# Splitting 784 token columns as 512 + 272 instead of 384 + 400 in the input projection of a hybrid encoder

## The chip, the cores and the metric

The kernel runs on one core of a Trainium2 chip. The metric is the device time of one execution in microseconds (us); the value for the kernel before is the median of three runs.

## The reference

One encoder layer is applied to two groups of tokens, a prompt of 1024 tokens and a sample of 256 tokens; each is preceded by the same 16 learned meta tokens. The model width is 2048, a head has 128 channels. All arrays are float32.

```python
u = rms_norm(h, norm_w) @ w_in                      # (tokens, 2048) x (2048, 6656)
qa, ka, va, za, qb, kb, vb, zb = jnp.split(u, split_points(), axis=-1)
qa = apply_axial_rope(rms_norm(qa, q_norm_a), rope_tabs)   # 8 heads
ka = apply_axial_rope(rms_norm(ka, k_norm_a), rope_tabs)   # 2 key/value heads
ya = global_gqa(qa, ka, va) * jax.nn.silu(za)
qb, kb = rms_norm(qb, q_norm_b), rms_norm(kb, k_norm_b)    # 8 heads
yb = neighbourhood_attention(qb, kb, vb, rpb) * jax.nn.silu(zb)
return h + jnp.concatenate([ya, yb], axis=-1) @ w_out      # (tokens, 2048) x (2048, 2048)
```

`global_gqa` is full softmax attention of one group over itself. `neighbourhood_attention` lets each token of a 64-column grid see a window of 8 rows by 16 columns with a learned bias, and the meta tokens.

## The kernel before, in words

**Number format.** Each float32 operand of a large product is split into two parts, a rounded high part and the rest, both of type float32r. A product is the sum of three matmuls: high times high, high times low, low times high. In the projection these are lines 199, 200 and 201 of `strips`, which take `wh` and `xh`, `wh` and `xl`, `wl` and `xh`. A weight tile of 128 x 128 is the stationary operand, a block of token columns of x the moving one, and the result goes to a PSUM tile (`pp`) with the 128 output channels on the partitions and the tokens along the row.

**Two chunks of tokens.** The 16 meta tokens, the 1024 prompt tokens and the 256 sample tokens are projected as two chunks. Chunk 1 holds 512 columns (256 of the sample, the first 240 of the prompt, 16 meta), chunk 2 the other T2 = 784 prompt tokens. Channels lie on the partitions, so an x tile is 128 channels by the chunk's tokens, and 16 such tiles (KT) make the 2048 channels.

**Strips.** The 6656 output channels are 52 strips of 128. `strips` projects one strip (or two together): for each of the 16 x tiles, for each block of token columns, three matmuls. In chunk 1 a strip has one block of 512 columns (keys, values) or of 496 (queries, gates, without the meta tokens). In chunk 2 a strip has two blocks, from the list `BL` in `chunk2`, and so two PSUM tiles of up to 512 columns:

```python
BL = [(0, NB), (NB, T2 - NB)]       # line 664; NB = 384: columns 0..384 and 384..784
```

When the strip is done, an evacuation reads both PSUM tiles, block after block: `qk_evac` (norm over the channels by an all-reduce on GpSimd, optional rope, split), `v_rows` and `rows_out` (128-column transposes on TensorE, copies, stores) or `z_evac` (silu). Intermediate tiles come from the pool `ev`, which has 8 buffers in chunk 2.

**x in chunk 2.** While chunk 1 is projected, the raw x of chunk 2 is copied to a DRAM buffer `x2d` and its squares are summed. `load_all_x` then opens chunk 2: for each of the 16 tiles one DMA on SP's queue (line 147) brings 784 columns into the place of the low part, ScalarE writes the high part (line 149), VectorE overwrites the place with the low part (line 150). The order of the tiles' places (3, 4, 0, 1, 2, 5, ...) follows the memory of chunk 1, which they take over. A tile is `[128, 2, 800]` with its start at a multiple of 128 bytes: the high part at column 0, the low part at column 800, and a block is the slice `xh[:, o:o + n]` or `xl[:, o:o + n]` of these.

**Order of the work.** Chunk 1 interleaves its strips with the attention of the sample. Chunk 2 runs the global heads first (for each head a gate strip, a query strip, four attention blocks of 256 queries, and one strip of the local heads as filling), then the other local strips between the blocks of the neighbourhood attention. The last four blocks run beside the beginning of the output projection, which works on two halves of 640 tokens as blocks of 320 columns (lines 915 to 917), and whose order is held as written. Elsewhere a planner with a timeline of estimated costs sets the order of the instructions on each engine, with a raised priority for the weight loads (`woff`); the DMAs of x in chunk 2 are held back behind the weight loads of the 48th strip (`early`).

Of the kernel before, what the change touches and what calls it, by code (L numbers as in the profile page):

```python
# [12 lines left out]
F32 = mybir.dt.float32  # L13
F32R = mybir.dt.float32r
AF = mybir.ActivationFunctionType
ALU = mybir.AluOpType
# [4 lines left out]
P = 128  # L21
DM = 2048
KT = 16
# [4 lines left out]
C1P = 240  # L28
T1 = NMETA + NS + C1P
T2 = NP - C1P  # L30
TX = 800
NB = 384
ALIGN = 128
NH = 8
EPS = 1e-6
# [13 lines left out]
class Kern:  # L49
# [39 lines left out]
    def get_x(self, kt):  # L89

        nc = self.nc
        if kt not in self.xs:
            for i in range(kt, kt + 3):
                self.load_x(i)
            r = self.xraw[kt]
            t = self.x.tile([P, 2, T1], F32R, tag="x", name="x", align_bytes=ALIGN)
            h, l = t[:, 0, :], t[:, 1, :]
            w = self.nw[:, kt:kt + 1]
            nc.scalar.activation(h, r, AF.Copy, scale=w)
            nc.vector.scalar_tensor_tensor(out=l, in0=r, scalar=w, in1=h.bitcast(F32), op0=ALU.mult, op1=ALU.subtract)  # L100
            if kt >= LAG:
                self.square(kt - LAG)
            self.xs[kt] = (h, l)
            if kt == KT - 1:
                for d, c in self.consts:
                    nc.sync.dma_start(d, c)
                nc.scalar.mul(self.nqkw[:], self.qkw[:], -1.0)
                for i in range(KT - LAG, KT):
                    self.square(i)
                self.token_scale(*self.scale, T1)  # L110
        return self.xs[kt]
# [26 lines left out]
    def load_all_x(self):  # L138


        nc = self.nc
        t = [self.x.tile([P, 2, TX], F32R, tag="x", name="x", align_bytes=ALIGN) for _ in range(KT)]
        for kt, i in enumerate((3, 4, 0, 1, 2, *range(5, KT))):
            h, l = t[i][:, 0, :T2], t[i][:, 1, :T2]
            r = l.bitcast(F32)
            with self.tc.issue_after(self.early):
                nc.sync.dma_start(r, self.x2d[kt][:])
            w = self.nw[:, kt:kt + 1]
            nc.scalar.activation(h, r, AF.Copy, scale=w)
            nc.vector.scalar_tensor_tensor(out=l, in0=r, scalar=w, in1=h.bitcast(F32), op0=ALU.mult, op1=ALU.subtract)  # L150
            self.xs[kt] = (h, l)
        for d, c in self.consts:
            nc.sync.dma_start(d, c)

# [11 lines left out]
    def strips(self, jobs, getx):  # L166


        nc, tc = self.nc, self.tc
        out = [[pool.tile([P, 512], F32, tag=tag, name="pp") for pool, tag in pools] for _, _, pools in jobs]  # L170
        for c in range(KT // WCH):
            ws = []
            for s, _, _ in jobs:
                with tc.high_priority(offset=self.woff):
                    w = self.raw.tile([P, WCH, P], F32, tag="raw", name="wr")
                    single = self.projected == 2 and c == 0 and not self.second
                    for i in range(0, WCH, 1 if single else WCH):
                        e = i + (1 if single else WCH)
                        self.lastw = nc.sync.dma_start(w[:, i:e], self.io["w_in"][s][:, c * WCH + i:c * WCH + e, :]).ins
                    wh = self.w.tile([P, WCH, P], F32R, tag="wh", name="wh")  # L180
                    wl = self.w.tile([P, WCH, P], F32R, tag="wl", name="wl")
                    if self.second and s not in AGAIN:
                        nc.sync.dma_start(wl[:].bitcast(F32), self.wld[s][:, c * WCH:(c + 1) * WCH, :])
                        nc.scalar.copy(wh[:], w[:])  # L184
                    else:
                        for i in range(0, WCH, 1 if single else WCH):
                            e = i + (1 if single else WCH)
                            self.lastsplit = self.split(wh[:, i:e], wl[:, i:e], w[:, i:e])
                            self.lasthi = self.hi
                ws.append((wh, wl))  # L190
                if not self.second and s not in AGAIN:
                    nc.sync.dma_start(self.wld[s][:, c * WCH:(c + 1) * WCH, :], wl[:].bitcast(F32))
            for k in range(WCH):
                kt = c * WCH + k
                xh, xl = getx(kt)
                for (wh, wl), ps, (_, blocks, _) in zip(ws, out, jobs):
                    for p, (o, n) in zip(ps, blocks):
                        first, last = kt == 0, kt == KT - 1
                        nc.tensor.matmul(p[:, :n], wh[:, k, :], xh[:, o:o + n], start=first, stop=False)  # L199
                        nc.tensor.matmul(p[:, :n], wh[:, k, :], xl[:, o:o + n], start=False, stop=False)  # L200
                        nc.tensor.matmul(p[:, :n], wl[:, k, :], xh[:, o:o + n], start=False, stop=last)  # L201
        return out

    def qk_evac(self, ps, o, n, wc, rope, segs):
# [266 lines left out]
    def rows_out(self, vt, n, dst, o):  # L471

        nc = self.nc
        for a in range(0, n, 4 * P):
            offs = range(a, min(n, a + 4 * P), P)
            full = [x for x in offs if x + P <= n]
            t = self.ev.tile([P, 3, P], F32, tag="ev", name="vl")
            tp = self.tp.tile([P, 4, P], F32, tag="tp", name="tp")
            for i, x in enumerate(offs):
                m = min(P, n - x)  # L480
                nc.tensor.transpose(tp[:m, i, :], vt[:, x:x + m], self.ident[:])
            f = len(full)
            nc.scalar.copy(t[:, :f, :], tp[:, :f, :])
            nc.sync.dma_start(dst[o + a:o + a + P * f].rearrange("(t p) d -> p t d", p=P), t[:, :f, :])
            if f < len(offs):
                m = n - offs[f]
                t = self.ev.tile([m, P], F32, tag="ev", name="vl")
                nc.scalar.copy(t[:], tp[:m, f, :])
                nc.sync.dma_start(dst[o + n - m:o + n], t[:])
# [165 lines left out]
    def chunk2(self):  # L655
# [7 lines left out]
        self.load_all_x()  # L663
        BL = [(0, NB), (NB, T2 - NB)]

# [491 lines left out]
```

## Time and profile before

| | |
|---|---|
| time, median of 3 runs | 2230.27 us (2229.54 to 2231.46) |
| profiled execution | 2232.76 us, of which its span is 2231.0 us |
| TensorE matmul busy | 2207.4 us, 99%, 13064 instructions |
| weight loads busy (beside the matmuls) | 2101.0 us, 94% |
| VectorE (DVE) busy | 1644.2 us, 74% |
| ScalarE (ACT) busy | 1127.5 us, 51% |
| GpSimd (POOL) busy | 531.2 us, 24% |
| DMA | 391.21 MB, mean 175 GB/s |
| granted TensorE clock, mean | 0.996 |

Busy time is the union of an engine's instructions as the profiler has them. Matmuls overlap: each is recorded from its start to the end of its last write, so a mean duration of 344 ns doesn't say that the next one starts 344 ns later. How fast TensorE goes is read from the start times in the timeline. In a group's row, "x832" is the number of instructions, the number after the bar is busy time in us and then the mean duration in ns, and after the second bar stand the idle time of the engine before them and what ended it. The span begins with chunk 1 (to about 625 us); chunk 2 lasts to about 1810 us, and the output projection ends the kernel.

### The profile page before, as it was taken

The numbers are of one execution on the slowest core, as the hardware profiler recorded it, in microseconds if no ns is written. First come the engines' busy times: TensorE is split into PE (matmuls) and PEld (weight loads), VectorE is DVE, ScalarE is ACT, GpSimd is POOL, SyncE is SP. The second block draws the span as 40 slices with busy tenths as digits, with TensorE's granted clock in tenths as the row PEclk, the third lists the DMA queues.
The fourth block names the chain that finished last, engine by engine and source line by source line (L and its number), as shares of the span: only waits on it lengthen the run. The fifth ranks groups of instructions, "written<-read, shape, count | busy, mean of one in ns | idle before, by whom it ended". The sixth has DMA issues, their size and how long they took to land.

```text
span 2231.0 us, 36738 instructions
## 1 busy us (share of the span) xinstructions
PE 2207.4 (99%) x13064; PEld 2101.0 (94%) x13064; DVE 1644.2 (74%) x2895; ACT 1127.5 (51%) x2288; POOL 531.2 (24%) x249
## 2 busy tenths in 40 slices
PE   8999999999999999999999999999999999999999
PEld 6888788888899999999999999999999999999999
DVE  7687876788855998994898998567668766536743
ACT  6555454455554676764676665444434454232220
POOL 1232421122211332331232233322422322000000
PEclk9999999999999999999999999999999999999999
DMA  8767899998464333334333336544343464745663
GB/s 287 222 192 223 272 310 312 323 299 297 143 219 144 101 104 114 95 118 140 101 106 114 105 110 206 158 139 143 117 132 109 136 221 140 230 148 161 201 211 111
DMA packets 267480, 391.21 MB, mean 175 GB/s; under 512 B 46720, under 2 KB 126496, under 8 KB 267296
## 3 DMA queue, kind: packets, MB, share of 16 engines
q1 hardware_dynamic: 267296, 388.86, 54.1%
q8 instruction: 102, 1.67, 0.3%
q14 instruction: 82, 0.67, 0.1%
HBM read 286.19 MB, written 102.42 MB: 174 GB/s over the span
## 4 chain that ended last, share of the span: by engine, by line
PE 89%; DVE 4%; DMA 3%; issue 1%; ACT 1%; SPq 1%; POOL 0%; DVEq 0%; ACTq 0%; POOLq 0%
PE pp L199 19%; PE pp L200 19%; PE pp L201 19%; PE pq L916 6%; PE pq L917 6%; PE pq L915 6%; PE po L460 2%; PE sp L321 1%; PE sp L322 1%; PE sp L323 1%; PE po L363 1%; PE po L361 1%; PE po L362 1%; DVE wl L56 1%; PE sp L428 1%
## 5 line engine op out<-in xcount | busy, mean ns | idle before, releaser
L199 PE MATMUL pp<-x,wh 128*128 128x384 f32 (+2 forms) x2496 | 896.3, 360 | 7.0 <-ACT wh L55 7.0
L200 PE MATMUL pp<-x,wh 128*128 128x384 f32 (+2 forms) x2496 | 893.7, 358 | 0.0
L201 PE MATMUL pp<-x,wl 128*128 128x384 f32 (+2 forms) x2496 | 889.3, 356 | 0.2 <-DVE wl L56 0.2
L199 PEld LDWEIGHTS pp<-x,wh 128*128 128x128 f32 x2496 | 469.6, 188 | 38.1 <-ACT wh L55 8.4
L201 PEld LDWEIGHTS pp<-x,wl 128*128 128x128 f32 x2496 | 470.2, 188 | 30.1 <-DVE wl L56 1.0
L200 PEld LDWEIGHTS pp<-x,wh 128*128 128x128 f32 x2496 | 470.1, 188 | 30.1 <-DVE x L150 0.5
L56 DVE TENSOR_TENSOR wl<-wr,wh 128x512 fp32r<-128x512 f32 (+1 forms) x402 | 288.6, 730 | 130.3 <-ACT wh L55 108.8
L55 ACT CAST wh<-wr 128x512 fp32r<-128x512 f32 (+1 forms) x402 | 239.7, 610 | 227.1 <-PE pp L200 164.8
L209 POOL PARTITION_ALL_REDUCE m<-ms x78 | 224.3, 2875 | 410.8 <-ACT ms L207 356.2
L290 POOL PARTITION_ALL_REDUCE tot<-a x80 | 186.7, 2334 | 469.7 <-DVE a L288 453.3
L916 PE MATMUL pq<-ym,wh 128*128 128x320 f32 x896 | 278.6, 311 | 2.0 <-DVE ym L56 1.9
L915 PE MATMUL pq<-ym,wh 128*128 128x320 f32 x896 | 278.8, 311 | 1.3 <-ACT ym L55 0.9
L917 PE MATMUL pq<-ym,wl 128*128 128x320 f32 x896 | 278.1, 310 | 0.0
L273 POOL PARTITION_ALL_REDUCE ma<-m x80 | 111.1, 1388 | 421.7 <-DVE m L271 419.1
L916 PEld LDWEIGHTS pq<-ym,wh 128*128 128x128 f32 x896 | 169.8, 189 | 2.8 <-DVE ym L56 2.8
L915 PEld LDWEIGHTS pq<-ym,wh 128*128 128x128 f32 x896 | 169.7, 190 | 2.2 <-ACT ym L55 1.5
L917 PEld LDWEIGHTS pq<-ym,wl 128*128 128x128 f32 x896 | 169.7, 189 | 0.3 <-DVE wl L56 0.3
L341 DVE TENSOR_TENSOR S<-S,ma 128x512 f32<-128x512 f32 x136 | 104.0, 820 | 8.1 <-POOL ma L273 7.7
L56 DVE TENSOR_TENSOR pl<-S,ph 128x512 fp32r<-128x512 f32 x136 | 100.1, 748 | 10.4 <-ACT ph L55 10.0
L325 ACT COPY S<-sp 128x512 f32<-128x512 f32 x136 | 78.1, 580 | 55.4 <-PE sp L323 42.5
L184 ACT CAST wh<-wr 128x512 fp32r<-128x512 f32 x132 | 81.3, 616 | 45.1 <-PE pp L200 43.4
L342 ACT ACTIVATE S<-S 128x512 f32<-128x512 f32 x136 | 83.6, 629 | 36.3 <-DVE S L341 36.2
(207 smaller groups left out, 3306.6 us busy)
## 6 DMA issues: line engine op xcount, KB each, us to landing
wr<-in_w_in SPq DMA_DIRECT2D x414, 256.0 KB, 3.7
wld<-wl SPq DMA_DIRECT2D x132, 256.0 KB, 4.5
wl<-wld SPq DMA_DIRECT2D x132, 256.0 KB, 3.2
wq<-in_w_out SPq DMA_DIRECT2D x64, 256.0 KB, 5.6
td<-wq SPq DMA_DIRECT2D x64, 256.0 KB, 4.3
wr<-td SPq DMA_DIRECT2D x64, 256.0 KB, 3.3
yr<-yd SPq DMA_DIRECT2D x48, 320.0 KB, 3.9
wr<-in_w_out SPq DMA_DIRECT2D x48, 256.0 KB, 4.1
```

What stands on the lines that cost most here:

```text
L55: self.hi = nc.scalar.copy(hi, full).ins
L56: return nc.vector.tensor_tensor(out=lo, in0=full, in1=hi.bitcast(F32), op=ALU.subtract).ins
L199: nc.tensor.matmul(p[:, :n], wh[:, k, :], xh[:, o:o + n], start=first, stop=False)
L200: nc.tensor.matmul(p[:, :n], wh[:, k, :], xl[:, o:o + n], start=False, stop=False)
L201: nc.tensor.matmul(p[:, :n], wl[:, k, :], xh[:, o:o + n], start=False, stop=last)
L209: nc.gpsimd.partition_all_reduce(m2[:], ms[:], P, RED.add)
L273: nc.gpsimd.partition_all_reduce(ma[:], m1[:], P, RED.max)
L290: nc.gpsimd.partition_all_reduce(tot[:], a1[:], P, RED.add)
L341: nc.vector.tensor_tensor(out=s, in0=s, in1=mb, op=ALU.subtract)
L915: nc.tensor.matmul(ps[:, b, :B], wh, yh[:, o], start=k == 0, stop=False)
L916: nc.tensor.matmul(ps[:, b, :B], wh, yl[:, o], start=False, stop=False)
L917: nc.tensor.matmul(ps[:, b, :B], wl, yh[:, o], start=False, stop=k == 7)
```

## The change

The two blocks of a strip in chunk 2 become 512 and 272 columns. A tile of x in chunk 2 is laid out by block: the high part of the first block at column 0, its low part at 512, the high part of the second at 1024, its low part at 1312; the row has 1584 columns instead of 1600. `load_all_x` makes each tile in two pieces, one per block, each with its own DMA, its own ScalarE copy and its own VectorE subtraction. `strips` takes a list of (high, low) pairs, one per block, instead of slicing by the offset. The tile into which `rows_out` copies its transposes holds four columns of 128 instead of three. The widest tile of the `ev` pool in chunk 2 goes from 400 columns to 512.

```diff
-TX = 800
-NB = 384
+NB = 512
+XLAY = ((0, 512, 512), (1024, 1312, 272))
+TX = 1584
...
-            self.xs[kt] = (h, l)
+            self.xs[kt] = [(h, l)]
...
-        t = [self.x.tile([P, 2, TX], F32R, tag="x", name="x", align_bytes=ALIGN) for _ in range(KT)]
+        t = [self.x.tile([P, TX], F32R, tag="x", name="x", align_bytes=ALIGN) for _ in range(KT)]
         for kt, i in enumerate((3, 4, 0, 1, 2, *range(5, KT))):
-            h, l = t[i][:, 0, :T2], t[i][:, 1, :T2]
-            r = l.bitcast(F32)
-            with self.tc.issue_after(self.early):
-                nc.sync.dma_start(r, self.x2d[kt][:])
             w = self.nw[:, kt:kt + 1]
-            nc.scalar.activation(h, r, AF.Copy, scale=w)
-            nc.vector.scalar_tensor_tensor(out=l, in0=r, scalar=w, in1=h.bitcast(F32), op0=ALU.mult, op1=ALU.subtract)
-            self.xs[kt] = (h, l)
+            self.xs[kt] = []
+            o = 0
+            for a, b, n in XLAY:
+                h, l = t[i][:, a:a + n], t[i][:, b:b + n]
+                r = l.bitcast(F32)
+                with self.tc.issue_after(self.early):
+                    nc.sync.dma_start(r, self.x2d[kt][:, o:o + n])
+                nc.scalar.activation(h, r, AF.Copy, scale=w)
+                nc.vector.scalar_tensor_tensor(out=l, in0=r, scalar=w, in1=h.bitcast(F32), op0=ALU.mult, op1=ALU.subtract)
+                self.xs[kt].append((h, l))
+                o += n
...
-                xh, xl = getx(kt)
+                x = getx(kt)
                 for (wh, wl), ps, (_, blocks, _) in zip(ws, out, jobs):
-                    for p, (o, n) in zip(ps, blocks):
+                    for p, (_, n), (xh, xl) in zip(ps, blocks, x):
                         first, last = kt == 0, kt == KT - 1
-                        nc.tensor.matmul(p[:, :n], wh[:, k, :], xh[:, o:o + n], start=first, stop=False)
-                        nc.tensor.matmul(p[:, :n], wh[:, k, :], xl[:, o:o + n], start=False, stop=False)
-                        nc.tensor.matmul(p[:, :n], wl[:, k, :], xh[:, o:o + n], start=False, stop=last)
+                        nc.tensor.matmul(p[:, :n], wh[:, k, :], xh[:, :n], start=first, stop=False)
+                        nc.tensor.matmul(p[:, :n], wh[:, k, :], xl[:, :n], start=False, stop=False)
+                        nc.tensor.matmul(p[:, :n], wl[:, k, :], xh[:, :n], start=False, stop=last)
...
-            t = self.ev.tile([P, 3, P], F32, tag="ev", name="vl")
+            t = self.ev.tile([P, 4, P], F32, tag="ev", name="vl")
```

## The prediction

> **What bounds the kernel now.** I read the page first: engine totals, the chain that ended last, and the costliest group.
>
> ```profile
> span 2231.0 us, 36738 instructions
> PE 2207.4 (99%) x13064; PEld 2101.0 (94%) x13064; DVE 1644.2 (74%) x2895; ACT 1127.5 (51%) x2288; POOL 531.2 (24%) x249
> ...
> PE 89%; DVE 4%; DMA 3%; issue 1%; ACT 1%; SPq 1%; POOL 0%; DVEq 0%; ACTq 0%; POOLq 0%
> ...
> L199 PE MATMUL pp<-x,wh 128*128 128x384 f32 (+2 forms) x2496 | 896.3, 360 | 7.0 <-ACT wh L55 7.0
> ```
>
> The tensor engine is named busy for 99% of the span and carries 89% of the last chain. "Busy" alone doesn't prove that it streams, since matmul ends are modelled. So I took the busy time of each engine by stage, and then the waits of PE inside the stretch where only the second chunk is projected and attended (650 to 1805 us).
>
> ```profile
> 620.00:650.00 30.00, 28.52 (x160) 27.28 (x158) 24.82 (x40) 21.93 (x36) 3.67 (x2) 0.94 0.90 321
> 650.00:700.00 50.00, 50.00 (x282) 49.90 (x282) 18.96 (x32) 19.48 (x38) 6.96 (x3) 1.00 0.44 138
> 700.00:1350.00 650.00, 650.00 (x4196) 648.29 (x4195) 563.25 (x1004) 426.89 (x879) 197.07 (x92) 1.00 0.36 112
> 1350.00:1805.00 455.00, 453.86 (x2763) 452.39 (x2762) 321.98 (x655) 204.13 (x445) 142.57 (x76) 1.00 0.44 138
> ```
> ```profile
> PE po L457 <- issue: 0.5, 1, 0.5
> PE po L457 <- DVE Pm L283: 0.3, 1, 0.3
> PE po L363 <- DVE pl L56: 0.3, 1, 0.3
> ```
>
> The columns of the first fence are the stretch, its length, then PE, weight loads, DVE, ACT and POOL busy (with instructions), the granted clock, DMA share and GB/s. From 650 to 1805 us PE waits for 1.1 us in total, at a granted clock of 1.00, while DVE is at 87% in the densest stretch (563.25 of 650). So in the second chunk the time is the number of matmuls times the distance from one start to the next. The change alters those distances and leaves their number as it is, so distances are what has to be priced.
>
> **The change: the matmuls.** These two groups (one of three lines each; the other two have the same counts) show what is replaced.
>
> ```profile
> L199 PE MATMUL pp<-x,wh 128*128 128x400 f32 x832 | 287.9, 346 | 0.0
> L199 PE MATMUL pp<-x,wh 128*128 128x384 f32 x832 | 286.6, 344 | 0.0
> ```
>
> 832 on each of L199, L200 and L201 gives 2496 matmuls of 384 columns and 2496 of 400. They become 2496 of 512 and 2496 of 272. The 344 and 346 ns are latencies, not prices; the price is read from start times in undisturbed stretches of the timeline. The rows below are, in order: chunk 2 (384/400), the last pair of strips of chunk 1 (496 and 512 in turn), a lone 496 strip, the output projection (320), the attention (256).
>
> ```profile
> 1020.48 0.34 PE L199 MATMUL pp<-x,wh 128*128 128x384 f32 x1
> ...
> 1022.64 0.34 PE L199 MATMUL pp<-x,wh 128*128 128x384 f32 x1
> ```
> ```profile
> 615.10 0.38 PE L199 MATMUL pp<-x,wh 128*128 128x496 f32 x1
> ...
> 615.76 0.39 PE L199 MATMUL pp<-x,wh 128*128 128x512 f32 x1
> ...
> 616.44 0.38 PE L199 MATMUL pp<-x,wh 128*128 128x496 f32 x1
> ```
> ```profile
> 70.83 0.38 PE L199 MATMUL pp<-x,wh 128*128 128x496 f32 x1
> ...
> 73.50 0.38 PE L199 MATMUL pp<-x,wh 128*128 128x496 f32 x1
> ```
> ```profile
> 1950.08 0.31 PE L915 MATMUL pq<-ym,wh 128*128 128x320 f32 x1
> ...
> 1951.84 0.31 PE L915 MATMUL pq<-ym,wh 128*128 128x320 f32 x1
> ```
> ```profile
> 1017.03 0.27 PE L363 MATMUL po<-pl,va 128*128 128x256 f32 x1
> ...
> 1017.73 0.28 PE L363 MATMUL po<-pl,va 128*128 128x256 f32 x1
> ```
>
> Between the two 384 rows lie two tiles of x, 12 matmuls: 2.16 us, that is 180.0 ns each and 360 ns for a 384 and a 400 together. Three matmuls of 496 take 0.66 us (220 ns each), three of 512 take 0.68 us (226.7 ns each). The lone 496 strip has 12 in 2.67 us (222.5 ns). Twelve of 320 take 1.76 us (146.7 ns), six of 256 take 0.70 us (116.7 ns).
>
> The line through 320 and 512 has a slope of 80.0 ns / 192 columns = 0.417 ns per column; with it 496 comes out at 220.0, as in the first 496 row, and 392 (the mean of today's blocks) at 176.7. Today's blocks cost 180.0, so they lie 3.3 ns per matmul above the line that three other widths keep. **This excess is all that the change can win on PE**: on the line the price is additive, and 512 + 272 costs what 384 + 400 would cost on it.
>
> A 272-column matmul isn't in the trace. Its bounds are the rows on both sides, 116.7 (256) and 146.7 (320); it is 16 columns from the first and 48 from the second. The line between these two gives 124.2, the line through 320 and 512 gives 126.7. I take 126.7, the dearer, because 256 lies a little under that line (120.0) and belongs to another kind of stage. Then 226.7 + 126.7 = 353.4 ns for a pair against 360, so 6.6 ns x 2496 = 16.5 us are saved; with 124.2 it is 9.1 ns, 22.7 us. With the raw ends it would be a gain of 41 us or a loss of 33 us (373.4 against 360).
>
> Here a rule speaks against any gain: the Trainium skill (TensorE: Matmul & The Clock Gate, section Back-to-back issue gap) gives N / 2.4 + 2.5 ns for the gap of a warm matmul, so both splittings of 784 columns would cost 331.7 ns (an estimate from that formula). Its slope, 0.417 ns per column, agrees with the trace; its constant doesn't (13.3 ns here), and it has no term for the excess of today's blocks.
>
> **The start of the second chunk.** `load_all_x` does each x tile in two pieces: 16 more DMA issues on SP, 16 more copies on ACT, 16 more subtractions on DVE, all in 620 to 650 us.
>
> ```profile
> L147 SPq DMA_DIRECT2D x<-x2d x16: 319/376/972, 619.8 to 638.0; - x16
> ```
> ```profile
> L149 ACT ACTIVATE x<-x,nw 128x784 fp32r<-128x784 f32 x16 | 14.6, 948 | 4.3 <-DMA x<-x2d 4.3
> L99 ACT ACTIVATE x<-xr,nw 128x512 fp32r<-128x512 f32 x16 | 11.2, 721 | 4.9 <-DMA xr<-in_x 4.9
> L55 ACT CAST qs<-rs_r 128x256 fp32r<-128x256 f32 x16 | 6.5, 407 | 23.8 <-DVE rs_r L223 16.7 <-DVE rs_r L225 7.0
> ```
> ```profile
> L150 DVE SCALAR_TENSOR_TENSOR x<-x,nw 128x784 fp32r<-128x784 f32 x16 | 16.5, 1051 | 3.1 <-ACT x L149 3.1
> L100 DVE SCALAR_TENSOR_TENSOR x<-xr,nw,x 128x512 fp32r<-128x512 f32 x16 | 11.7, 746 | 7.8 <-ACT x L99 7.6
> L307 DVE SCALAR_TENSOR_TENSOR y<-y,r 128x256 f32<-128x256 f32 x80 | 39.1, 489 | 1.5
> ```
>
> ACT: 721 + about 420 (407 for 256 columns) against 948, so 0.19 us x 16 = 3.1 us more. DVE: 746 + about 500 (489 for 256) against 1051, 0.20 x 16 = 3.1 us more. SP: 16 x 0.376 = 6.0 us more of issuing, behind which the weight loads of the next strips queue. The cover is the idle time of 620 to 650 us: DVE has 5.2 us left, ACT 8.1. It just suffices, and the 512-column piece of each tile is ready earlier than the whole is today, which is a gain. Bounds: -1 to +6 us; I take +1, nearer to the cover that exists.
>
> **The evacuations.** Each strip is still read out in two blocks by the same operations; only their widths move. Prices are nearly straight in the width:
>
> ```profile
> L62 ACT ACTIVATE rs_l<-m 128x400 f32<-128x400 f32 x26 | 13.9, 536 | 21.7 <-DVE m L210 21.7
> L62 ACT ACTIVATE rs_l<-m 128x384 f32<-128x384 f32 x26 | 13.6, 525 | 50.5 <-DVE m L210 50.5
> ...
> L62 ACT ACTIVATE rs_l<-m 128x512 f32<-128x512 f32 x10 | 6.3, 631 | 11.9 <-DVE m L210 11.9
> ```
>
> 525 + 536 = 1061 ns on ACT today; 631 + about 430 after. The first block's chain gets longer and the second's shorter; PE has another strip or attention block beside it, and without that cover the longer chain would cost up to 0.1 us per operation and strip. I put it at nothing. The transposes and copies of `rows_out` keep their counts (3 + 4 transposes become 4 + 3). What can eat into the gain is DVE: with PE 1% faster its share of 700 to 1350 us rises from 87% to 88%, and the order on each engine is planned anew; I take 1 us for this.
>
> **Sum.** 16.5 - 1 - 1 = 14.5 us off. The profiled execution took 2232.76 us, its span 2231.0, with 1.8 us around it; its own time becomes 2218.3. It lies 2.5 us above the median of 2230.27, so on the median's scale the forecast is 2216.
>
> **The rivals.** (1) The excess stays. Today's pair has a width that is an odd multiple of 16 (400), and 272 is one too; the lone strip of 496, another, runs at 222.5, above the line. If what costs 3.3 ns per matmul is this, or unequal blocks in turn, the new pair costs 360 as well. For it: today's only alternating pair in chunk 2 is at 180.0 in the rows above. Against it: 496 and 512 in turn keep the line exactly. Result: 2230.3 + 1 = 2231.
>
> (2) The 272-column matmul is dear; this one ends slower. Each matmul has its own weight load, and a short matmul leaves less room for the next load. The place is all 2496 narrow matmuls, the point from which it decides is 360 - 226.7 = 133.3 ns. At 140, half way to the 320 row from there, the pair costs 366.7, 6.7 x 2496 = 16.7 us more: 2247. For it: loads are recorded as busy for 49.90 of 50 us in 650 to 700. Against it: with 256 columns the same loads fit into 116.7.
>
> (3) The start of the chunk stalls. If the 6.0 us of issues land on PE whole, and the streaming gain is absent, the result is 2236; with the full gain it would be 2221, still faster.
>
> **How the numbers follow.** What a measurement of this kernel can tell from no change is about 0.2%, 4.5 us. Chances: forecast 0.62, (1) 0.19, (2) 0.10, (3) without the gain 0.09. The forecast is faster beyond 4.5 us; (1) is within it but for 0.02; (3) is slower but for 0.01; (2) is slower. So faster 0.62, same 0.18, slower 0.20. The range goes from 2209 (272 at 124.2, nothing lost elsewhere, 21 us) to 2236 (case 3); case (2) and a little below the low end are left out. The likeliest case's own range is 2209 to 2222.
>
> **What would show it.** In the timeline of the changed kernel, 12 matmuls in an undisturbed stretch of chunk 2 should take 6 x 353.4 = 2.12 us: three of 512 in 0.68, three of 272 in 0.38. A sum of 1.08 us for these six, as today, is rival 1; clearly more than 0.40 for the three of 272 is rival 2. PE's busy time in 650 to 1805 us should stay whole with a stage shorter by some 16 us, and the waits of PE there about 1 us. In the start stage, more than 3 us of new PE idle time or a longer stretch below full clock means rival 3. The forecast is wrong if the distances shrink as said and PE meanwhile gains waits on DVE or ACT in the attention stages.

## The result and the profile after

The changed kernel takes 2221.48 us (median of 8 runs, 2219.8 to 2224.84), beside 2229.9 us (8 runs, 2225.83 to 2232.34) for the kernel before on the same chip: a ratio of 0.9966, 95% interval 0.9955 to 0.9977, or 8.4 us less. It is faster by the bound of 0.2%. The forecast was 2216 us, with a gain of 14.5 us; the sign and the mechanism came as forecast, the size is a little over half; the time lies just inside the likeliest case's own range, 2209 to 2222 us.

The profiled execution took 2220.95 us. The page of the changed kernel, in the lines that were shown of before:

```profile
span 2219.1 us, 36801 instructions
PE 2194.2 (99%) x13064; PEld 1982.6 (89%) x13064; DVE 1646.5 (74%) x2911; ACT 1130.9 (51%) x2304; POOL 523.9 (24%) x249
...
PE 91%; DVE 3%; DMA 3%; issue 1%; ACT 1%; POOL 0%; SPq 0%; DVEq 0%; POOLq 0%; ACTq 0%
...
L204 PE MATMUL pp<-x,wh 128*128 128x512 f32 (+1 forms) x2496 | 890.3, 358 | 9.1 <-ACT wh L56 6.3
```

The same 13064 matmuls, the same 99%, 11.9 us less span. Work by stretch of the changed kernel (columns as before), then the waits of PE that are new or answer to those of before:

```profile
620.00:650.00 30.00, 27.27 (x147) 22.89 (x147) 24.66 (x52) 24.50 (x51) 3.25 (x2) 0.94 0.88 293
650.00:700.00 50.00, 50.00 (x287) 44.14 (x286) 20.04 (x34) 19.21 (x38) 7.65 (x3) 1.00 0.48 148
700.00:1350.00 650.00, 650.00 (x4215) 594.54 (x4214) 556.45 (x1000) 428.30 (x877) 187.65 (x93) 1.00 0.37 112
1350.00:1795.00 445.00, 444.69 (x2741) 401.08 (x2740) 329.97 (x659) 202.53 (x447) 145.87 (x76) 1.00 0.45 141
```
```profile
PE po L462 <- DVE Pm L288: 0.3, 1, 0.3
PE pp L204 <- ACT x L153: 2.7, 3, 1.6
```

PE is whole from 650 us on, in a stage that is shorter, and its wait there is 0.3 us. More matmuls fit in 700 to 1350 us (4215 for 4196). What is new stands in the first stretch: 2.7 us in which PE waits for ScalarE's high parts of x. Weight loads are recorded as busy for 594.54 of 650 us instead of 648.29. That alone doesn't make matmuls cheaper: a kernel below (f1) has them busy for 647.55 us of this stretch, and its undisturbed tiles there run as fast as those of the changed kernel.

The stages are bounded by two starts in the timeline, the first matmul of chunk 2 and the first of the output projection; before, then after:

```profile
625.19 1.34 PE L199 MATMUL pp<-x,wh 128*128 128x384 f32 x3
...
1810.81 0.41 PE L915 MATMUL pq<-ym,wh 128*128 128x320 f32 x1
```
```profile
622.52 0.50 PE L204 MATMUL pp<-x,wh 128*128 128x512 f32 x1 [1.60 <-ACT x L153]
...
1800.11 0.41 PE L920 MATMUL pq<-ym,wh 128*128 128x320 f32 x1 [0.38 <-ACT ym L56]
```

Chunk 2 takes 1185.6 us before and 1177.6 after, **8.0 us less**. The other 3.9 us of the two spans lie in chunk 1 (2.7) and the output projection (1.2), whose work the change leaves as it is. Single executions differ by that: over the kernels below, with the same chunk 1, chunk 2 begins between 621.4 and 626.2 us. The medians' 8.4 us agrees with chunk 2 alone. I split chunk 2 over the distances from each matmul's start to the next one's. What exceeds 0.417 ns per column + 13.3 ns by over 45 ns counts as stall, the rest as the matmul's price (matmuls of fewer than 256 columns, which all belong to the attention or to transposes, count whole as price):

| chunk 2, us | before | after |
|---|---|---|
| 4992 projection matmuls | 896.7 | 887.6 |
| other matmuls, of the attention above all | 280.3 | 280.7 |
| stalls (of them before 700 us) | 8.6 (2.1) | 9.2 (3.9) |

So everything came out of the projection's distances, 9.1 us, and 1.8 us of stalls at the start of the chunk were paid for it; other stalls fell by 1.2.

Four rows of the changed kernel's timeline in an undisturbed stretch, and five right after the attention:

```profile
690.59 0.39 PE L204 MATMUL pp<-x,wh 128*128 128x512 f32 x1
691.28 0.29 PE L204 MATMUL pp<-x,wh 128*128 128x272 f32 x1
691.65 0.39 PE L204 MATMUL pp<-x,wh 128*128 128x512 f32 x1
...
692.71 0.39 PE L204 MATMUL pp<-x,wh 128*128 128x512 f32 x1
```
```profile
1412.70 0.65 PE L465 MATMUL po<-S,vw 128*128 128x192 f32 x3
...
1414.01 0.40 PE L204 MATMUL pp<-x,wh 128*128 128x512 f32 x1
...
1415.11 0.39 PE L204 MATMUL pp<-x,wh 128*128 128x512 f32 x1
...
1416.17 0.39 PE L204 MATMUL pp<-x,wh 128*128 128x512 f32 x1
...
1417.23 0.39 PE L204 MATMUL pp<-x,wh 128*128 128x512 f32 x1
```

In the first fence two tiles of x take 2.12 us: 1060 ns for six matmuls, 353.3 for a pair, as forecast. In the second the first whole tile after the attention takes 1.10 us, the next two 1.06. Over all 2496 pairs the mean is 355.6 ns, not 353.3, and before it was 359.3, not 360.0.

### The profile page after: what moved, and what is told of

The parts are those of the page before. It is cut to its first block, busy times and chain, and to the rows that moved or that the text cites. A ratio compares the mean times of both kernels' runs of the same rounds, so it can differ in the third digit from the quotient of the medians.

```text
span 2219.1 us, 36801 instructions
## 1 busy us (share of the span) xinstructions
PE 2194.2 (99%) x13064; PEld 1982.6 (89%) x13064; DVE 1646.5 (74%) x2911; ACT 1130.9 (51%) x2304; POOL 523.9 (24%) x249
## 4 chain that ended last, share of the span: by engine, by line
PE 91%; DVE 3%; DMA 3%; issue 1%; ACT 1%; POOL 0%; SPq 0%; DVEq 0%; POOLq 0%; ACTq 0%
PE pp L204 20%; PE pp L206 20%; PE pp L205 20%; PE pq L921 6%; PE pq L922 6%; PE pq L920 6%; PE po L465 2%; PE sp L328 1%; PE sp L327 1%; PE sp L326 1%; PE po L368 1%; PE po L366 1%; PE po L367 1%; DVE wl L57 1%; DMA wr<-in_w_in 1%
## 5 line engine op out<-in xcount | busy, mean ns | idle before, releaser
L204 PE MATMUL pp<-x,wh 128*128 128x512 f32 (+1 forms) x2496 | 890.3, 358 | 9.1 <-ACT wh L56 6.3
L206 PE MATMUL pp<-x,wl 128*128 128x512 f32 (+1 forms) x2496 | 890.5, 357 | 0.0
L205 PE MATMUL pp<-x,wh 128*128 128x512 f32 (+1 forms) x2496 | 887.7, 356 | 0.0
L214 POOL PARTITION_ALL_REDUCE m<-ms x78 | 231.6, 2969 | 405.8 <-ACT ms L212 368.4
L295 POOL PARTITION_ALL_REDUCE tot<-a x80 | 181.8, 2273 | 472.6 <-DVE a L293 456.6
L278 POOL PARTITION_ALL_REDUCE ma<-m x80 | 101.5, 1268 | 424.8 <-DVE m L276 423.5
L346 DVE TENSOR_TENSOR S<-S,ma 128x512 f32<-128x512 f32 x136 | 98.4, 779 | 8.8 <-POOL ma L278 8.8
L56 ACT CAST ph<-S 128x512 fp32r<-128x512 f32 x136 | 83.4, 615 | 33.2 <-PE po L367 32.2
```

The costliest lines, as they stand in the source:

```text
L56: self.hi = nc.scalar.copy(hi, full).ins
L204: nc.tensor.matmul(p[:, :n], wh[:, k, :], xh[:, :n], start=first, stop=False)
L205: nc.tensor.matmul(p[:, :n], wh[:, k, :], xl[:, :n], start=False, stop=False)
L206: nc.tensor.matmul(p[:, :n], wl[:, k, :], xh[:, :n], start=False, stop=last)
L214: nc.gpsimd.partition_all_reduce(m2[:], ms[:], P, RED.add)
L278: nc.gpsimd.partition_all_reduce(ma[:], m1[:], P, RED.max)
```

## The experiments

All times below are medians, and the ratios are to runs of the kernel before on the same chip: it took 2228.44 us beside e1 to e4, 2230.35 beside f1 to f4, 2229.41 beside g1 to g3 and 2229.48 beside h1. "Six" is the time of an undisturbed tile of x (six matmuls; from the fifth tile after an interruption on), "projection" the sum over the 4992 matmuls of chunk 2 as in the table above (one profiled execution each).

| | time, us | ratio, 95% interval | six, ns | projection, us | start stalls, us |
|---|---|---|---|---|---|
| before | 2229.9 | | 1076 and 1084 in turn | 896.7 | 2.1 |
| after | 2221.48 | 0.9966, 0.9955 to 0.9977 | 1060 | 887.6 | 3.9 |
| e1 widths only | 2222.65 | 0.9972, 0.9961 to 0.9982 | 1073.3 | 891.7 | 2.4 |
| e2 layout only | 2226.14 | 0.9987, 0.9977 to 0.9998 | 1073.3 | 893.7 | 4.2 |
| e3 384 + 416 | 2243.84 | 1.0068, 1.0051 to 1.0085 | 1093.3 | 910.1 | 4.1 |
| e4 two tiles in turn | 2220.22 | 0.9960, 0.9945 to 0.9975 | 1066.7 | 888.5 | 4.0 |
| f1 384, by block, 256 B | 2225.38 | 0.9983, 0.9973 to 0.9993 | 1060 or 1086.7 | 891.7 | 4.1 |
| f2 512, by block, 256 B | 2221.27 | 0.9962, 0.9949 to 0.9975 | 1060 or 1073.3 | 888.9 | 4.1 |
| f3 384, old layout, 256 B | 2225.57 | 0.9985, 0.9975 to 0.9995 | 1060 or 1086.7 | 892.6 | 3.0 |
| f4 512, old layout, 256 B | 2220.49 | 0.9962, 0.9950 to 0.9974 | 1060 or 1073.3 | 888.9 | 2.8 |
| g1 attention, 256 B | 2218.88 | 0.9953, 0.9940 to 0.9967 | 1060 | 887.6 | 3.4 |
| h1 wide low part odd | 2224.81 | 0.9980, 0.9968 to 0.9992 | 1073.3, some 1066.7 | 892.7 | 3.9 |

### Is it the widths or the layout?

The first runs take the two halves of the change apart. **e1** is the kernel before with other blocks, x in one piece as before:

```diff
-NB = 384
+NB = 512
...
-            t = self.ev.tile([P, 3, P], F32, tag="ev", name="vl")
+            t = self.ev.tile([P, 4, P], F32, tag="ev", name="vl")
```

> Blocks of 512 and 272 in the old layout of x (high part at column 0, low part at 800, one DMA, one copy and one subtraction per tile). Theory W (the widths set the price of a strip): the three 512 and three 272 of an x tile take 1060 ns in an undisturbed stretch, as in the changed kernel, the projection of chunk 2 sums to about 888 us, and the start of the chunk is as before; 2220 us. Rival L (the place of the parts sets it: in the old layout the first low part starts at an odd multiple of 128 bytes): the six take about 1080 ns, the projection of chunk 2 about 897 us; 2229 us.

**e2** is the changed kernel with the old widths:

```diff
-NB = 512
-XLAY = ((0, 512, 512), (1024, 1312, 272))
+NB = 384
+XLAY = ((0, 384, 384), (768, 1184, 400))
```

> Blocks of 384 and 400 as before, x laid out by block and loaded in two pieces per tile. Theory W: six matmuls of an x tile keep 1076 to 1084 ns, the projection of chunk 2 keeps 897 us, and the two-piece start costs 0 to 2 us: 2230 to 2232 us. Rival L: the six fall to 1060 ns, projection about 887 us, 2221 us.

In the timelines of e1 and e2, two tiles of x lie between the two rows:

```profile
689.72 0.40 PE L199 MATMUL pp<-x,wh 128*128 128x512 f32 x1
...
691.87 0.40 PE L199 MATMUL pp<-x,wh 128*128 128x512 f32 x1
```
```profile
689.84 0.34 PE L204 MATMUL pp<-x,wh 128*128 128x384 f32 x1
...
691.98 0.34 PE L204 MATMUL pp<-x,wh 128*128 128x384 f32 x1
```

Both take 2146.7 ns for two tiles in the trace's exact starts, 1073.3 for six: between the 1060 that one theory wanted and the 1080 of the other, in both kernels. Neither theory holds alone. Each half of the change takes away a part of the excess, and each half leaves 13.3 ns. Of the 9.1 us that the projection lost, the widths alone bring 5.0 (e1), the layout alone 3.0 (e2).

**e3** tests the first rival's reason, that 400 and 272 as odd multiples of 16 are what costs. It is e2 with 16 zero columns behind the 400, which are multiplied too:

```diff
+PAD = 416
...
+                if n == T2 - NB:
+                    h, l = t[i][:, a:a + PAD], t[i][:, b:b + PAD]
+                    for v in (h, l):
+                        nc.gpsimd.memset(v[:, n:].bitcast(F32), 0.0)
...
+                        if self.second and n == T2 - NB:
+                            n = PAD
```

> As the layout-only kernel, but the second block of a strip multiplies 416 columns instead of 400; the 16 columns added are zeros and their sums are not read. On the line through 320 and 512 columns a 384 and a 416 cost 360.0 ns together. Theory O (the 400, no multiple of 32 columns, pays for being one; a width that is a multiple of 32 stays on the line): six take 1080 ns, no more than today's with 400, and the time stays at 2230 us although 2496 matmuls stream 16 columns more. Rival U (any unequal pair of such widths pays 3 ns per matmul): 1100 ns, 16 us more, 2246 us.

```profile
689.83 0.35 PE L211 MATMUL pp<-x,wh 128*128 128x416 f32 x1
...
692.02 0.35 PE L211 MATMUL pp<-x,wh 128*128 128x416 f32 x1
```

Two tiles take 2.19 us, six 1093.3 ns: 20.0 more than in e2 for 3 x 16 columns, so 0.417 ns per column, the line's slope, and the 13.3 ns of e2 stay. An even multiple of 16 costs its columns and wins nothing: that theory falls.

**e4** halves the changes of width: for two tiles of x first the six matmuls of 512, then the six of 272.

```diff
+            G = 2 if self.second else 1
...
+                    for b, (p, (_, n)) in enumerate(zip(ps, blocks)):
+                        for g in range(G):
```

> The changed kernel, but in chunk 2 a strip does a block for two x tiles before the next block: six matmuls of 512, then six of 272, half as many changes of width. Theory T (in steady flow the pair is on the line at 353.3 ns whatever the order, and what lifts the mean to 355.7 are the first two x tiles after each return from attention matmuls): twelve take 2120 ns when undisturbed, the mean over chunk 2 stays at 355 to 356, 2221 us. Rival S (each change of width costs): the mean falls by half of the excess, 1.2 ns x 2496 = 3 us, 2218 us.

```profile
1744.87 0.28 PE L208 MATMUL pp<-x,wh 128*128 128x272 f32 x1
...
1747.01 0.28 PE L208 MATMUL pp<-x,wh 128*128 128x272 f32 x1
```

Two tiles take 2133.3 ns, 13.3 more than in the changed kernel, although widths change half as often; the mean pair is 356.0 and the time the same within its interval. That each change of width costs something is therefore not the explanation.

### Where the operands begin

All excesses so far are 13.3 ns (in e4 over two tiles) or, before, 20 on the mean. The kernels also differ in where a block begins in memory. With 4 bytes per column, and the x tiles themselves at multiples of 256 B in all of them, the low part of the first block stands at 3200 B in before and e1 (25 x 128, odd), at 2048 or 1536 B in after, e2 and e3 (even); the low part of the second block at an odd multiple in all five (4736 B, 37 x 128, under 400 columns; 5248 B, 41 x 128, under 272). The next four kernels put every part at a multiple of 256 B, each width in each layout:

```diff
f1:  NB = 384   XLAY = ((0, 384, 384), (768, 1216, 400))    TX = 1616   align_bytes=256
f2:  NB = 512   XLAY = ((0, 512, 512), (1024, 1344, 272))   TX = 1616   align_bytes=256
f3:  kernel before                                          TX = 832    align_bytes=256
f4:  e1                                                     TX = 832    align_bytes=256
```

> Blocks of 384 and 400, x by block in two pieces as in the layout-only kernel (six matmuls of an x tile: 1073 ns, of which 13 ns lie above the line), but the low part of the second block moved from an odd to an even multiple of 128 bytes, so that all four parts start at multiples of 256 bytes; x tiles at multiples of 256 bytes too. Theory M (the excess is paid where a moving operand starts at another phase of 256 bytes than its neighbours): six matmuls fall to 1060 ns, projection of chunk 2 from 893.7 to 882 to 886 us, 2217 us. Rival V (384 and 400 as widths pay 13 ns wherever the parts lie): 1073 ns as before, 2226 us.

> The changed kernel with the low part of its second block moved likewise to a multiple of 256 bytes. Theory M: undisturbed x tiles keep 1060 ns, and the first two x tiles after a return from attention (1092 and 1067 ns) fall towards 1060; projection 882 to 886 us instead of 887.6, 2217 to 2220 us. Rival T (the returns themselves cost, whatever the places): nothing changes, 887.6 us, 2221 us.

> The kernel before with one number changed in effect: the low parts of x start at column 832 instead of 800 (a multiple of 256 bytes), x tiles at multiples of 256 bytes; blocks of 384 and 400, one load per tile. Theory M: six matmuls fall from 1076 to 1084 to 1060 ns, projection from 896.7 to 882 to 886 us; 2216 us, as fast as or faster than the changed kernel without its new widths. Rival V: 1073 ns or more, 2226 to 2230 us.

> Blocks of 512 and 272 in the old layout with the low parts at column 832, one load per tile. Theory M: six matmuls fall from the 1073 ns of the widths-only kernel to 1060, projection from 891.7 to 882 to 886 us, start of the chunk without the two-piece loads; 2216 us. Rival V: 1073 ns, 2223 us.

With 512 and 272 in the old layout, the move alone takes the projection from 891.7 (e1) to 888.9 us (f4), and the six from 1073.3 to 1060 ns in 148 of f4's 211 undisturbed tiles: the layout by block isn't needed for it. In the other 63 tiles, as in 62 of the 202 of f2, 1069, 1085 and 1066 ns follow each other over and over, 1073.3 on the mean. Three such tiles of f2 lie between these rows, 3.22 us:

```profile
684.50 0.39 PE L204 MATMUL pp<-x,wh 128*128 128x512 f32 x1
...
687.72 0.39 PE L204 MATMUL pp<-x,wh 128*128 128x512 f32 x1
```

With 384 and 400 there are two lasting states too, here in f1's timeline, 12 matmuls between the rows of each fence:

```profile
1744.69 0.33 PE L204 MATMUL pp<-x,wh 128*128 128x384 f32 x1
...
1746.81 0.33 PE L204 MATMUL pp<-x,wh 128*128 128x384 f32 x1
```
```profile
1765.09 0.35 PE L204 MATMUL pp<-x,wh 128*128 128x400 f32 x1
...
1767.26 0.35 PE L204 MATMUL pp<-x,wh 128*128 128x400 f32 x1
```

2.12 us in one, 2.17 in the other (1060 and 1086.7 for six), in one and the same kernel. From the fifth tile after an interruption on, about three quarters of the tiles are in the first in f1, two thirds in f3. Apart from its first tile, no uninterrupted run of tiles goes from one of the two to the other. So with all starts at multiples of 256 B both pairs of widths run at the line in about two thirds of the undisturbed tiles, and fall off it for whole stretches: 384 and 400 by 26.7 ns, 512 and 272 by 13.3. The changed kernel, whose one odd start is the low part of the 272 block, is at 1060 in all of its 202.

**h1** makes the counter-test: the changed kernel with the low part of the 512 block at an odd multiple of 128 B (4480) and that of the 272 block at an even one:

```diff
-XLAY = ((0, 512, 512), (1024, 1312, 272))
-TX = 1584
+XLAY = ((0, 1120, 512), (832, 512, 272))
+TX = 1632
...
-        t = [self.x.tile([P, TX], F32R, tag="x", name="x", align_bytes=ALIGN) for _ in range(KT)]
+        t = [self.x.tile([P, TX], F32R, tag="x", name="x", align_bytes=256) for _ in range(KT)]
```

> The changed kernel with the parts of an x tile in other places: the low part of the 512 block now starts at an odd multiple of 128 bytes (column 1120), the low part of the 272 block at an even one (column 512); tiles at multiples of 256 bytes. In the changed kernel it is the other way round, in the widths-only kernel both are odd. Theory P (an odd start costs where the operand is the wide one, and nothing where it is the 272): undisturbed x tiles take 1073 ns, as in the widths-only kernel; projection of chunk 2 about 891 us, 2223 us. Rival Q (one odd part alone costs nothing, it takes two): 1060 ns, 887.6 us, 2221 us.

```profile
1749.85 0.39 PE L204 MATMUL pp<-x,wh 128*128 128x512 f32 x1
...
1752.00 0.39 PE L204 MATMUL pp<-x,wh 128*128 128x512 f32 x1
```

2.15 us for two tiles again, 1073.3 for six (in 165 of 202 undisturbed tiles; 1066.7 in the others) and 892.7 us of projection. The ratio's interval overlaps that of after (0.9968 to 0.9977), so the difference rests on the distances. The odd start under the wide block costs 13.3 ns in most tiles; the same start under the 272 block costs nothing (after: 1060). This one was expected and came. An odd start isn't the only source of such an excess, though: f2 and f4 have none and pay the same 13.3 ns in part of their tiles.

### What a return from the attention costs

**g1** sets the attention's tiles (`q`, `ph`, `pl`, `S`) to 256 B, to see whether the start of what comes between sets the price of the return; **g2** and **g3** put three matmuls of 256 columns with zero weights behind the x tiles 4, 8 and 12 of a strip (153 insertions), reading x from column 0 or from column 32 (128 B); each ran once, in 2281.18 and 2278.42 us:

```diff
+                if self.second and kt in (3, 7, 11):
+                    for _ in range(3):
+                        nc.tensor.matmul(out[0][0][:, :256], self.zero[:], x[0][0][:, :256], start=False, stop=False)    # g3: 32:288
```

> The changed kernel with the moving operands of the attention (q, the two parts of the probabilities, the scores) moved from odd multiples of 128 bytes to multiples of 256, the phase that the x parts have. Theory M (a change of phase between neighbouring moving operands is what costs at a return from attention to the projection): the x tiles after a return fall from 1092 and 1067 ns to about 1060, the projection of chunk 2 from 887.6 to about 882 us, 2216 us. Rival T (the return itself costs, some 17 ns on the mean of 340 returns, whatever the phase): 887.6 us, 2221 us.

> The changed kernel with three matmuls of 256 columns put in after the 4th, 8th and 12th x tile of each strip of chunk 2; their weights are zeros, so nothing is added to the sums; they read the first x part from its start (a multiple of 256 bytes). 156 insertions of about 354 ns: 55 us, and 6 us if each return costs 39 ns; about 2282 us. Theory T: the x tiles after an insertion take 1092 and 1067 ns, or 39 ns over 1060 in other portions. Theory M: they stay at 1060.

> As the kernel with insertions, but the inserted matmuls read the first x part from its column 32 (an odd multiple of 128 bytes). Theory T: as there, 39 ns over 1060 per insertion. Theory M: here, and only here, the two x tiles after an insertion cost 39 ns more together.

```profile
670.57 0.52 PE L209 MATMUL pp<-x,zero 128*128 128x256 f32 x3
...
675.21 0.28 PE L209 MATMUL pp<-x,zero 128*128 128x256 f32 x1
```
```profile
666.44 0.52 PE L209 MATMUL pp<-x,zero 128*128 128x256 f32 x3
...
671.08 0.28 PE L209 MATMUL pp<-x,zero 128*128 128x256 f32 x1
```

A cycle of four tiles and one insertion takes 4.64 us in both; four times 1060 and three times 120.0 make 4.60. In such a stretch an insertion costs 40 ns beyond its own columns, wherever it reads (in 26 of 34 such cycles of each kernel). Over all 153 the mean is smaller: price without stalls rises over after by 56.7 and 57.3 us, 11 and 14 ns each beyond 360. And g1's projection is 887.6 us, as in after. So the price of a return doesn't hang on where the attention's tiles begin, and an interruption without any attention has a price too; what in an interruption costs, no run separates. g1 has the lowest ratio of all, but its interval overlaps that of after (0.9940 to 0.9967 beside 0.9955 to 0.9977), and its projection isn't shorter: it is not shown to be faster. No kernel here is.

## Why the prediction was right, and where it was short

**The bound.** That PE streams in chunk 2 and distances set the time held: the stage became shorter by 8.0 us with PE whole and 0.3 us of waits. VectorE took 556.45 of 650 us (86%) where 88% was forecast; the 1 us kept for planning and DVE was not needed.

**The price of a pair.** 353.4 ns was forecast for an undisturbed pair, 353.3 measured (1060 / 3). Inside it the terms lie a little otherwise: the 512s take 232, 224 and 231 ns (229 on the mean for 226.7), the 272s 124.3 (for 126.7).

**The term that was too large** is "6.6 ns x 2496 = 16.5 us": it gave every pair the price of undisturbed ones, on both sides. The means over chunk 2 are 359.3 and 355.6 ns. Measured against 2496 x 353.3 = 881.9 us, before had an excess of 14.8 us, not the 16.5 assumed (0.7 ns less a pair, some 2 us), and after still has 5.7 us. That is 16.5 - 2 - 5.7, about 9 us, and 9.1 was measured. The 5.7 us belong to the matmuls beside the attention: there are 340 returns, 17 ns each on the mean, like the 1.10 us tile in the second timeline above. By the starts in the trace of after, 2.8 us lie in the first six matmuls after a return, 1.4 in the next six, 0.9 in the third six and 0.4 in the last one before an attention block; the other 1800 or so hold 0.2. The working used only rows of undisturbed stretches. In chunk 2 of the trace of before the price can't be seen, since the first six matmuls after a return lie 2.7 ns each above the line there and the undisturbed ones 3.3. In chunk 1 it can: the first three after a return lie 4.7 ns above it, those from the 25th on 1.2.

**The start of the chunk**: +1 forecast within -1 to +6, +1.8 measured. By-form rows of ScalarE in 615 to 655 us of the changed kernel:

```profile
L153 ACT ACTIVATE x<-x,nw 128x512 fp32r<-128x512 f32 x16 | 11.6, 724 | 2.8 <-DMA x<-x2d 2.8
L153 ACT ACTIVATE x<-x,nw 128x272 fp32r<-128x272 f32 x16 | 8.4, 523 | 0.5 <-DMA x<-x2d 0.5
```

The 512 piece is as forecast (721), the 272 piece took 523 ns instead of about 420 (an estimate), so ScalarE has 4.8 us more (724 + 523 - 948, times 16) instead of 3.1. Kernels that load x in two pieces have 1.1 to 2.0 us more stall there than their one-piece partners (after and e1, f2 and f4, f1 and f3, e2 and before).

**The rivals.** (1) The excess stays: no for this change, but it had a part of the truth. Not the odd multiple of 16 (e3), nor the unequal turn as such (after runs on the line), but the excess does depend on something besides the widths, as e1 and h1 show: with the wide low part at an odd start, 512 and 272 keep 13.3 ns a tile. With that the forecast was luckier than its reasons: it took width alone to be the cause, and width alone brings 5.0 of the 9.1 us (e1). The new layout put the wide low part at an even start, which the prediction didn't weigh. (2) A dear 272: no, 124.3 ns where 133.3 was the break-even. (3) The start: 1.8 us, below the 3 us named as its sign.

**The rule weighed.** The formula of the Trainium skill (TensorE: Matmul & The Clock Gate, section Back-to-back issue gap) would have both splittings equal. The section gives it for an isolated matmul and says that in a stream of weight loads and matmuls both set the distance, which the prediction left out. Its slope agrees with e3 less e2 (20.0 ns for 48 columns); that splittings come out equal does not agree with before and after (1080 and 1060 for six).

## What to carry to other kernels

Where PE streams, price matmuls by the distances of their starts, over the whole stage and not only in its calm stretches: a tile after an interruption can cost more than its widths say, and what a steady flow gains is partly paid back there. Before changing block widths, look at where each moving operand begins: here 512 and 272 lost 13.3 ns per tile of six matmuls with the wide block's low part at an odd multiple of 128 B, and a few columns of padding took that away in 70% of the undisturbed tiles (f4). Even starts everywhere are no guarantee, so read the distances again after the move. And one load cut in two cost 1 to 2 us of stalls at the head of its stage, so a layout that gives the same starts with one load is worth trying first.

## What the hardware showed that I had not expected

- The excess of an undisturbed tile over the line is a whole multiple of 6.7 ns on the mean: 0 (after, g1), 6.7 (e4, some tiles of h1), 13.3 (e1, e2, e3, h1, part of f2 and f4), 20 (before, 1076 and 1084 in turn), 26.7 (part of f1 and f3); an insertion in a calm stretch costs 40.
- The same instructions with the same operands have two lasting rates: 1060 and 1086.7 ns (f1, f3), 1060 and 1073.3 (f2, f4), 1066.7 and 1073.3 (h1). A tile of x settles into one of them within a few tiles of an interruption and stays there until the next. What in TensorE or its weight loads holds a state isn't shown by any run here.
- Why 384 and 400 lose twice as much in their second state as 512 and 272, why the odd start under the 272 block goes with no second state at all, and why e4's longer turn costs 13.3 ns per two tiles in steady flow, stays open.
